# Fox layer of a two-layer trunk: the residual turned by VectorE's 32x32 blocks and transfers through DRAM, and added by VectorE, in place of transposes on TensorE

## The chip, the cores and the metric

The kernel runs on one core of one Trainium2 chip. The metric is the device time of one execution in microseconds (us), the median of several executions. The profile is of one further execution; its times count from the start of its span.

## What is computed

The reference is a decoder trunk of two pre-norm residual layers on a sequence of 1024 positions with 1024 features, all in float32: an RG-LRU layer, then an attention layer with a forget gate ("FoX"), then a final RMSNorm. What matters here is the end:

```python
def fox_mixer(h, w_in, b_f, w_out):
    ...                      # q, k, v, gate; softmax with a decay; o = p @ v per head
    y = o * jax.nn.silu(gate)
    return y @ w_out.astype(h.dtype)

x = x + fox_mixer(h, ...)    # second layer; x is the residual after the first
return rms_norm(x, final_g)  # over the features of each position
```

## The kernel before, in words

**Layout.** Through both layers the features lie on the 128 partitions and the positions run along a partition (`x` is held as 8 blocks `db` of 128 features, each for two halves `c` of 512 positions). The output is wanted the other way round, a position on a partition, so that the final norm sums along the partition. A product that must be exact to float32 is three matmuls of rounded parts (high times high, low times high, high times low): `hh`/`hl` and `wh`/`wl` are the high and low parts of an activation and of a weight.

**The attention layer.** The loop of lines 1127 to 1177 goes over 16 heads. For each half `c`, `maxima` (line 752) makes the scores `S` on TensorE, VectorE subtracts the mask and takes the row maximum, ScalarE takes the exponential; `weigh` (line 817) turns the weights (`pt`, on TensorE for the last heads), ScalarE and VectorE split them into `ph` and `pl`, and TensorE multiplies them with `v` into `O`. The sums of a head pass through DRAM: `rc` to `recd` (line 796), back broadcast to `recb` (line 805). GpSimd multiplies them into the gate (`scale`, line 810) and the gate into the head (`gated`, line 909), and `split_y` (line 986) splits the gated head.

**The output projection.** `y` has 8 blocks of 128 features, one for each pair of heads. The first 6 blocks are multiplied with `w_out` beside heads 14 and 15 by `partial` (line 1005): for each feature block `db` and half `c`, 16 in all, it loads the residual block `xp` from `x1d` in DRAM, makes a product of 18 matmuls in a PSUM bank (`ops` in the profile), has VectorE add the two (line 1016), and stores the sum over the residual in `x1d` (line 1017). The order is (db, c) = (0,0) (1,0) (0,1) (1,1) (2,0) ... (6,0) (7,0) (6,1) (7,1). The tag `R` has two buffers, so each `xp` is loaded when the store from the last but one is through.

The last two blocks wait for heads 12 to 15, and come out in the other layout: `turned` (line 1036) makes, for each of 8 blocks of 128 positions and 2 halves `h` of 512 features, a PSUM bank (`turn`) in which 4 transposes of the residual (`x`, loaded by `residual`, line 1023) and 6 matmuls with `y` as the stationary part are summed. These are 16 groups: 8 for c=0, of which three run among the last matmuls of head 15, and then 8 for c=1. For c=0 all groups use the two banks of tag `g`, which the `ops` use too; for c=1 the blocks alternate between the tags `g` and `O`, two banks each. Behind a group ScalarE squares and sums it (line 1066) and VectorE multiplies it with the gain `grow` (lines 1068, 1071). For c=1 each block's root mean (`root_mean`, line 1080) is taken at once and the block is scaled, half on ScalarE, half on VectorE (lines 1072, 1073); for c=0 `finish` (line 1192) takes one root for all four blocks and scales them beside the groups of c=1.

**What sets the order.** Each engine has one queue in order. The strings `ORDER` and `LAST` (lines 27, 28) and those in `run` say how the steps of a head (digits) and of the projection (dots, `fill`) are woven on TensorE; a scheduler then places every engine's instructions by its own estimate of times. All DMAs are issued by SyncE, in order: an issue that waits holds up those behind it.

## Time and profile before

| | |
|---|---|
| time, median of 3 runs | 1112.8 us (1111.73 to 1114.34) |
| profiled execution | 1113.33 us, its span 1111.6 us |
| TensorE matmul busy | 1088.2 us, 98% of the span |
| VectorE busy | 785.4 us, 71% |
| ScalarE busy | 581.3 us, 52% |
| GpSimd busy | 175.2 us, 16% |
| DMA | 145.8 MB, mean 131 GB/s |

The profiler's page names engines PE (TensorE), PEld (its weight loads, beside the matmuls), DVE (VectorE), ACT (ScalarE), POOL (GpSimd) and SP (SyncE). A row of the timeline is start, duration, engine, line, operation, output<-inputs, shape, and in brackets the idle time before it and what ended it. Matmuls follow one another before the row of the one ahead ends, so durations of matmuls overlap and what counts is the distance of their starts. A "line" can be that of a helper: all matmuls stand at line 57, all splits at lines 87 (high) and 98 (low). The granted clock is 1.00 from start to end but for the last 3 us.

### The profile page before, as it was taken

How to read it: one execution, taken by the hardware profiler on the slowest of the kernel's cores; microseconds unless marked ns; L12 is line 12 of the kernel's file. 1: busy time of each engine (PE TensorE's matmuls, PEld its weight loads, DVE VectorE, ACT ScalarE, POOL GpSimd, SP SyncE). 2: the span in 40 equal slices, each digit the busy share in tenths (PEclk: the TensorE clock that was granted, in tenths of full speed). 3: DMA queues.
4: the chain of work that ended last, by engine and by line, in shares of the span. 5: the costliest groups of instructions: out<-in, count | busy, mean ns of one | idle time of the engine just before them, and what ended most of it. 6: DMA issues, size and time to landing. Idle time of an engine off the chain costs nothing.

```text
span 1111.6 us, 15903 instructions
## 1 busy us (share of the span) xinstructions
PE 1088.2 (98%) x5645; PEld 921.9 (83%) x5645; DVE 785.4 (71%) x1280; ACT 581.3 (52%) x1037; POOL 175.2 (16%) x120
## 2 busy tenths in 40 slices
PE   9999999999999999999999999999999999999997
PEld 7787888888888888988888888888888889888876
DVE  7888755876568687757788477875678765666645
ACT  8487345355453665545555355553555544444435
POOL 2322212111212201420010200202002020110110
PEclk9999999999999999999999999999999999999999
DMA  6111111111112113446767347675376763885445
GB/s 220 62 52 43 51 54 48 43 54 45 49 45 75 48 55 127 130 113 165 199 204 195 116 139 195 198 198 146 107 204 195 202 170 100 251 294 182 138 148 189
DMA packets 100919, 145.81 MB, mean 131 GB/s; under 512 B 25348, under 2 KB 53636, under 8 KB 100840
## 3 DMA queue, kind: packets, MB, share of 16 engines
q1 hardware_dynamic: 100840, 144.80, 44.2%
q8 instruction: 44, 0.72, 0.3%
q14 instruction: 35, 0.29, 0.1%
HBM read 83.48 MB, written 36.11 MB: 108 GB/s over the span
## 4 chain that ended last, share of the span: by engine, by line
PE 75%; DMA 8%; DVE 7%; issue 5%; ACT 3%; SPq 1%; POOL 1%; ACTq 0%; DVEq 0%; POOLq 0%
PE gps L57 24%; PE ops L57 16%; PE ups L57 10%; PE vps L57 8%; PE O L57 5%; PE S L57 4%; PE gate L57 3%; PE turn L57 2%; DMA pp<-turnd 2%; PE pt L61 2%; DMA wf<-in_w 2%; DVE pl L98 2%; DMA turnd<-turn 1%; DVE turn L735 1%; DVE S L775 1%
## 5 line engine op out<-in xcount | busy, mean ns | idle before, releaser
L57 PE MATMUL gps<-hh,wh 128*128 128x512 f32 x576 | 229.8, 399 | 0.3 <-ACT wh L87 0.3
L57 PE MATMUL gps<-hh,wl 128*128 128x512 f32 x576 | 226.2, 393 | 0.0
L57 PE MATMUL gps<-hl,wh 128*128 128x512 f32 x576 | 225.3, 391 | 0.0
L87 ACT CAST wh<-wf 128x512 fp32r<-128x512 f32 (+2 forms) x156 | 94.5, 610 | 152.6 <-PE gps L57 47.8
L98 POOL TENSOR_TENSOR wl<-wf,wh 128x512 fp32r<-128x512 f32 (+1 forms) x60 | 101.9, 1705 | 376.0 <-ACT wh L87 261.4
L57 PEld LDWEIGHTS gps<-hl,wh 128*128 128x128 f32 x576 | 108.5, 188 | 23.5
L57 PEld LDWEIGHTS gps<-hh,wl 128*128 128x128 f32 x576 | 108.8, 189 | 19.6 <-POOL wl L98 0.2
L57 PEld LDWEIGHTS gps<-hh,wh 128*128 128x128 f32 x576 | 108.7, 189 | 19.4 <-ACT wh L87 0.6
L815 POOL TENSOR_TENSOR sg<-sg,recb 64x512 f32<-64x512 f32 x32 | 44.1, 1397 | 494.9 <-DMA recb<-recd 494.9
L775 DVE CUSTOM_DVE_ANT_0 S<-S,mask 128x512 f32<-128x512 f32 (+7 forms) x128 | 97.1, 758 | 25.4 <-PE S L57 24.9
L780 ACT ACTIVATE pp<-S,m 128x512 f32<-128x512 f32 (+1 forms) x64 | 54.4, 850 | 76.8 <-DVE m L775 76.3
L57 PE MATMUL S<-T,U 128*128 128x512 f32 (+7 forms) x384 | 91.4, 346 | 0.0
L57 PE MATMUL O<-pl,v 128*128 128x256 f32 (+3 forms) x302 | 80.3, 301 | 10.8 <-DVE pl L98 10.5
L98 DVE TENSOR_TENSOR wl<-wf,wh 128x512 fp32r<-128x512 f32 x96 | 64.9, 677 | 30.7 <-ACT wh L87 30.5
L375 DVE TENSOR_TENSOR x<-x,ops 128x512 f32<-128x512 f32 x80 | 54.1, 680 | 40.7 <-PE ops L57 40.7
L57 PE MATMUL O<-ph,v 128*128 128x256 f32 (+3 forms) x302 | 80.1, 289 | 1.3 <-ACT ph L87 1.3
L57 PEld LDWEIGHTS S<-T,U 128*128 128x128 f32 (+1 forms) x384 | 68.2, 189 | 12.6 <-ACT pp L780 0.6
L57 PE MATMUL ups<-hh,wl 128*128 128x512 f32 x192 | 75.3, 392 | 0.8 <-POOL wl L98 0.8
L57 PE MATMUL ups<-hh,wh 128*128 128x512 f32 x192 | 75.5, 394 | 0.4 <-ACT hh L89 0.4
L57 PE MATMUL ops<-yh,wh 128*128 128x512 f32 x192 | 75.2, 392 | 0.0
L57 PE MATMUL ups<-hl,wh 128*128 128x512 f32 x192 | 75.1, 391 | 0.1
L57 PE MATMUL ops<-yh,wl 128*128 128x512 f32 x192 | 74.7, 389 | 0.0
(170 smaller groups left out, 2361.8 us busy)
## 6 DMA issues: line engine op xcount, KB each, us to landing
wf<-in_w SPq DMA_DIRECT2D x100, 256.0 KB
turnd<-turn SPq DMA_DIRECT2D x26, 448.0 KB
pp<-turnd SPq DMA_DIRECT2D x52, 224.0 KB
wf<-in_wo SPq DMA_DIRECT2D x64, 128.0 KB
U<-qkh SPq DMA_DIRECT2D x64, 128.0 KB
T<-qkh SPq DMA_DIRECT2D x28, 256.0 KB
turnd<-turn SPq DMA_DIRECT2D x13, 384.0 KB
pp<-turnd SPq DMA_DIRECT2D x52, 96.0 KB
```

The source lines that it names most:

```text
L57: pe[0] = nc.tensor.matmul(*args, **kw)
L61: pe[0] = nc.tensor.transpose(*args)
L87: nc.scalar.copy(hi, src)
L98: return eng.tensor_tensor(lo, src, f32(hi), ALU.subtract)
L375: nc.vector.tensor_tensor(x, x, pt, ALU.add)
L735: nc.vector.transpose(t[:, 0 if c else r].rearrange("p (m k q) -> p k m q", m=4, q=32), p[:, :n].rearrange("p (k m q) -> p k m q", m=4, q=32),
L775: masked[0] = nc.vector.tensor_tensor_reduce(S[:, :n], S[:, :n], mask[:, SEQ - n :], -1.0, -NEG, ALU.add, ALU.min, accum_out=m)
L780: seen[0] = nc.scalar.activation(p, S[:, :n], AF.Exp, bias=m, scale=-1.0, accum_out=sums[:, i : i + 1])
L815: nc.gpsimd.tensor_tensor(sg, sg, recs[hd // 2][rows, part], ALU.mult)
```

## The change

`partial` no longer stores the sum in the old layout. VectorE adds the residual to the product in the PSUM bank itself, then turns it by its transpose of 32x32 blocks into the tile `x`, and four stores of 64 KB put the blocks into a new DRAM tensor `x2d` such that a position's row of features can be read back onto a partition. `fetch` loads them, 512 KB at a time, four for each half `c`; `fetch(0)` is placed ahead of the last product, `fetch(1)` behind head 15.

`turned` makes the bank of 6 matmuls alone; VectorE then adds the residual piece by piece (two additions of 256 columns for a group), from PSUM and SBUF into `res`. The square of ScalarE reads `res`. For c=0 the product with the gain goes to GpSimd, and `finish` scales one half on ScalarE, one on VectorE. For c=1 VectorE applies root and gain in one instruction for each half (line 1105 of the changed kernel). The last block of c=1 (`early`) is an exception: there TensorE adds the residual with an identity matrix in float32 (two matmuls of 256 columns for a group), and the rest is as before. The gain `grow` lies in two tiles of another pool, and its load stands earlier in SyncE's queue. The diff, cut to its core:

```diff
+    x2d = dram.tile([2, P, KT, 4, P], F32, name="x2d")
...
+                if (db, c) == todo[-1]:
+                    fetch(0)
...
-                nc.vector.tensor_tensor(x, x, pt, ALU.add)
-                nc.sync.dma_start(x1d[c, :, db], x)
+                nc.vector.tensor_tensor(pt, x, pt, ALU.add)
+                nc.vector.transpose(
+                    x.rearrange("p (b k d) -> p k b d", b=4, d=32), pt.rearrange("p (k b q) -> p k b q", b=4, q=32)
+                )
+                for m in range(4):
+                    nc.sync.dma_start(
+                        x2d[c, :, db, m].rearrange("(b q) f -> q b f", b=4),
+                        x[32 * m : 32 * m + 32].rearrange("q (b f) -> q b f", b=4),
+                    )
...
+        def fetch(c):
+            if c == 0:
+                x = [tu.tile([P, SEQ], F32, tag=t, name="x1") for t in ("U", "U0", "U1")]
+                x.append(at.tile([P, SEQ], F32, tag="sg", name="x1"))
+            else:
+                x = [tu.tile([P, 2, SEQ], F32, tag=f"T{h}", name="x1") for h in range(2)]
+                x = [z[:, i] for z in x for i in range(2)]
+            for d, z in enumerate(x):
+                nc.sync.dma_start(z, x2d[c, :, 2 * d : 2 * d + 2].rearrange("p e m f -> p (e m f)"))
+            rows_of[c] = x
...
-                    for i in range(4):
-                        x = xs[4 * h + i][:, b * P : (b + 1) * P]
-                        matmul(pt[:, i * P : (i + 1) * P], x, ident, start=i == 0, stop=False, is_transpose=True)
+                    pt = bank(b)
+                    if early:
+                        for i, (x, p) in enumerate(pieces(c, b, h, pt)):
+                            matmul(p, ident, x, start=i == 0, stop=False)
...
+                    src = pt
+                    if not early:
+                        src = res[h]
+                        for x, o, p in pieces(c, b, h, src, pt):
+                            nc.vector.tensor_tensor(o, x, p, ALU.add)
...
-                    nc.scalar.activation(sq, pt, AF.Square, accum_out=ss[:, h : h + 1])
+                    nc.scalar.activation(sq, src, AF.Square, accum_out=ss[:, h : h + 1])
+                    if c == 0:
+                        nc.gpsimd.tensor_tensor(src, src, grow[h], ALU.mult)
...
+                else:
+                    r = root_mean(ss)
+                    for z, g_ in zip(res, grow):
+                        nc.vector.scalar_tensor_tensor(z, z, r, g_, ALU.mult, ALU.mult)
...
-                nc.vector.tensor_scalar(o, o, r[:, i : i + 1], None, ALU.mult)
-                nc.sync.dma_start(out[i], o)
+                nc.scalar.activation(res[0], res[0], AF.Copy, scale=r_)
+                nc.vector.tensor_scalar(res[1], res[1], r_, None, ALU.mult)
+                for o, hs in zip(res, halves):
+                    nc.sync.dma_start(out[i, :, hs], o)
```

**VectorE around the last product.** `ops_10356` is the last product before, (7,1); the lines are: 906 a head's halves added, 98 a low part, 1016 the sum with the residual, 1068 the product with the gain.

```order
L906 TENSOR_TENSOR yo<-yo,O 64x256
L98 TENSOR_TENSOR yhl<-yo,yhh 128x256
L1016 TENSOR_TENSOR xp<-xp,ops_10356 128x512
L1068 TENSOR_TENSOR res<-turn,grow 128x512
L98 TENSOR_TENSOR pl<-pt,ph 128x512 x2
L1068 TENSOR_TENSOR res<-turn,grow 128x512
```

In the changed kernel the same product is `ops_10427`; the lines 907, 1019 stand for 906, 1016, line 1020 is the new transpose, line 1086 a new addition of 256 columns.

```order
L907 TENSOR_TENSOR yo<-yo,O 64x256
L98 TENSOR_TENSOR yhl<-yo,yhh 128x256
L1019 TENSOR_TENSOR ops_10427<-xp,ops_10427 128x512
L1020 STREAM_TRANSPOSE xp<-ops_10427 128x4x4x32
L1086 TENSOR_TENSOR res<-x_10417,turn 128x256
L1086 TENSOR_TENSOR res<-x_10418,turn 128x256
L1086 TENSOR_TENSOR res<-x_10419,turn 128x256
L1086 TENSOR_TENSOR res<-x_10420,turn 128x256
L98 TENSOR_TENSOR pl<-pt,ph 128x512 x3
```

The transpose, which reads the bank, stands behind the sum, and the additions of the first two groups stand ahead of the low parts `pl` where one product with the gain stood.

**VectorE at the end**, before, from the root of c=0 (`ssq_4013`) on; `ssq_4014` are the sums of c=1, line 1087 the reciprocal of a root, line 1073 a scaling by it.

```order
L1087 RECIPROCAL ssq_4013<-ssq_4013 128x4
L1197 TENSOR_SCALAR res<-res,ssq_4013 128x1024 x4
L1068 TENSOR_TENSOR res<-turn,grow 128x512
L1084 TENSOR_TENSOR ssq_4014<-ssq_4014 128x1
L1071 TENSOR_TENSOR res<-turn,grow 128x512
L1068 TENSOR_TENSOR res<-turn,grow 128x512
L1087 RECIPROCAL ssq_4014<-ssq_4014 128x1
```

The changed kernel's last rows; there `ssq_4015` are the sums of c=1, line 1105 is the scaling by root and gain, lines 1092, 1099 and 1101 belong to the last block.

```order
L1086 TENSOR_TENSOR res<-x_10624,turn 128x256 x2
L1114 TENSOR_TENSOR ssq_4015<-ssq_4015 128x1 x2
L1117 RECIPROCAL ssq_4015<-ssq_4015 128x1
L1105 SCALAR_TENSOR_TENSOR res<-res,ssq_4015,grow 128x512 x2
L1092 TENSOR_TENSOR res<-turn,grow 128x512
L1117 RECIPROCAL ssq_4015<-ssq_4015 128x1
L1114 TENSOR_TENSOR ssq_4015<-ssq_4015 128x1
L1099 TENSOR_TENSOR res<-turn,grow 128x512
L1105 SCALAR_TENSOR_TENSOR res<-res,ssq_4015,grow 128x512 x2
L1117 RECIPROCAL ssq_4015<-ssq_4015 128x1
L1101 TENSOR_SCALAR res<-res,ssq_4015 128x512
```

The scalings of the third block stand among the last block's instructions, ahead of its reciprocal.

**SyncE's queue around head 15's last sums**, before: line 1013 loads a residual block, line 1017 stores a sum, lines 1029 and 1033 load the residual for the groups.

```order
L1017 DMA x1d<-xp 128x512
L1013 DMA xp<-x1d 128x512
L1029 DMA x_10390<-x1d 128x256
L1033 DMA x_10582<-x1d 128x2x256
L796 DMA recd<-rc 4x128
L1033 DMA x_10514<-x1d 128x2x256
L805 DMA recb<-recd 64x512
```

And in the changed kernel, where line 1016 loads a residual block, line 1024 stores a turned sum, and line 1042 is `fetch`, with `x_10417` to `x_10420` for c=0 and `x_10623`, `x_10624` for c=1.

```order
L1024 DMA x2d<-xp 32x4x128 x4
L1042 DMA x_10419<-x2d 128x1024
L1042 DMA x_10624<-x2d 128x1024
L1016 DMA xp<-x1d 128x512
L1024 DMA x2d<-xp 32x4x128 x4
L797 DMA recd<-rc 4x128
L1042 DMA x_10420<-x2d 128x1024
L1016 DMA xp<-x1d 128x512
L806 DMA recb<-recd 64x512
L1024 DMA x2d<-xp 32x4x128 x8
L1042 DMA x_10624<-x2d 128x1024
```

Ahead of `recb` there now stand a fetch of 512 KB and a load, which wait for the four stores before them.

More of the change, by code (lines that the diff above doesn't have):

```diff
@@ new lines, in turned, with bank @@
+        def turned(c):
+            def bank(b):
+                return ps.tile([P, HALF], F32, tag="gO"[c * (b % 2)], name="turn")
+            homes = [(wpool, t) for t in ("wl", "wh") * 4]
+            if c:
+                homes = [(rpool, "R")] * 2 + [(at, t) for t in ("ph", "pl") * 3]
+            for b in range(4):
+                cs = slice(b * P, (b + 1) * P)
+                ss = ssq[c][:, 2 * b : 2 * b + 2]
+                early = c == 1 and b == 3
+                res = []
+                for h, hs in enumerate(halves):
+                    own, tag = homes.pop(0)
+                    kw = dict(bufs=3) if own is at else {}
+                    res.append(own.tile([P, HALF], F32, tag=tag, name="res", **kw))
+                    pt = bank(b)
+                    if early:
+                        for i, (x, p) in enumerate(pieces(c, b, h, pt)):
+                            matmul(p, ident, x, start=i == 0, stop=False)
@@ L1059, in turned @@
                         wh, wl = (z[:, k::2] for z in late_w[h])
-                        matmul(pt, yh, wh, start=False, stop=False)
+                        matmul(pt, yh, wh, start=k == 0 and not early, stop=False)
                         matmul(pt, yl, wh, start=False, stop=False)
@@ L1188, in trunk @@
         drain(fill)
-        for q in range(2):
-            left[1, q] = residual(1, q)
+        fetch(1)
         def finish():
```

64 lines of the change are left out of this document (25 added, 39 removed).

## The prediction

> **What bounds the kernel now.** I read the busy time by stage first, then TensorE's waits, then the chain that ended last, then the timeline of the last 50 us. Columns of the stages: length, and busy us (instructions) of PE, PEld, DVE, ACT and POOL, then granted clock, DMA share and GB/s.
>
> ```profile
> 480.00:960.00 480.00, 467.41 (x2685) 403.80 (x2684) 343.31 (x667) 243.30 (x530) 60.28 (x42) 1.00 0.63 171
> 960.00:1070.00 110.00, 110.00 (x571) 93.37 (x570) 65.37 (x132) 47.74 (x101) 10.24 (x8) 1.00 0.63 206
> ```
>
> From 960 to 1070 us, where the sixteen `ops1` products run beside heads 14 and 15, TensorE has no idle time at all and VectorE is busy 65.4 of 110 us. After 1070 the rest of the output projection runs in 16 groups (8 for c=0, 8 for c=1), each 4 transposes and 6 matmuls. There TensorE waits once, in the list of its waits from 960 us on:
>
> ```profile
> PE turn L57 <- DVE xp L1016: 1.7, 1, 1.7
> ```
>
> The chain of waits says what that wait hangs on (start, us, what), and how the end follows:
>
> ```profile
> 1064.31 3.51 DMA recd<-rc
> ...
> 1067.84 2.73 DMA recb<-recd
> ...
> 1073.72 0.70 DVE xp L1016
> ...
> 1074.46 1.35 PE turn L57 x7
> ...
> 1082.94 22.71 PE turn L57 x123
> ...
> 1107.32 0.72 ACT res L1072
> ```
>
> The softmax sums of head 15 travel through DRAM and land at 1070.57, GpSimd and ScalarE use them, VectorE splits the gated head, and only behind that in VectorE's order comes the addition that empties the PSUM bank of the last `ops1`. From 1074.46 on TensorE runs without a pause to 1105.64, and 6.0 us of tail (squares, root, scaling, transfer) follow to 1111.6. So 31 us are bound by TensorE, behind one fixed start.
>
> **What the change takes from TensorE.** The timeline of c=0's last groups, a row for each matmul:
>
> ```profile
> 1087.18 0.60 PE L57 MATMUL turn<-ident,x 128*128 128x128 f32 x4
> 1087.54 0.48 PE L57 MATMUL turn<-woh,yhh 128*128 128x512 f32 x1
> ...
> 1089.01 0.60 PE L57 MATMUL turn<-ident,x 128*128 128x128 f32 x4
> ...
> 1090.84 0.60 PE L57 MATMUL turn<-ident,x 128*128 128x128 f32 x4
> ```
>
> A group takes 1.83 us. Its 4 transposes take 0.36, and the first matmul behind them is some 0.08 late; six matmuls alone take 1.40. So 0.43 us go from each of 14 groups, 6.0 us. The last two groups keep the residual on TensorE, as two fp32 matmuls of 256 columns in place of four transposes. The nearest row is the fp32 matmul of 512 columns, two instructions, up to the start of what follows:
>
> ```profile
> 34.75 1.02 PE L57 MATMUL rsrow<-rs,onesf 128*128 128x512 f32 x2
> 35.61 0.95 PE L57 MATMUL sscol<-onesf,m 128*128 128x1 f32 x8
> ```
>
> That is 0.86 for 512 columns, so 0.86 for twice 256: 0.43 more than the transposes, 0.9 us for the two groups. TensorE's own saving is 5.1 us. What of it arrives at the end is the question.
>
> **What comes in ahead.** Sixteen VectorE transposes of 128x512 between 980 and 1075 us. The rows of the same operation at other lengths, and of the additions and scalings used below (busy, mean ns):
>
> ```profile
> L735 DVE STREAM_TRANSPOSE turn<-pp 128x896 f32<-128x896 f32 x26 | 28.8, 1110 | 8.3 <-ACT pp L780 8.1
> L735 DVE STREAM_TRANSPOSE turn<-pp 128x384 f32<-128x384 f32 x26 | 14.8, 568 | 2.1 <-ACT pp L780 2.1
> L98 DVE TENSOR_TENSOR wgl<-wgf,wgh 128x256 fp32r<-128x256 f32 x12 | 5.0, 414 | 0.0
> L1073 DVE TENSOR_SCALAR res<-res,ssq 128x512 f32<-128x512 f32 x4 | 1.9, 486 | 0.1
> ```
>
> A straight line through the first two gives 0.70 us at 512. That is 11.2 us more for VectorE, whose share in the stage goes from 0.59 to 0.70. TensorE waits on none of it directly; it would wait on what stands behind a transpose in VectorE's order, the low parts `pl`, the row maxima, the banks. The tightest place that I found is this: `pl` is done at 1000.82 and read at 1002.45.
>
> ```profile
> 1000.27 0.55 DVE L98 TENSOR_TENSOR pl<-pt,ph 128x384 fp32r<-128x384 f32 x1
> 1002.45 0.28 PE L57 MATMUL O<-ph,v 128*128 128x256 f32 x1
> ```
>
> Two transposes stand ahead of it in the new order, so some 1.1 to 1.4 us of the 1.6 are used up. The cost lies between 0 and 2.9 us: the stage 480 to 960, with VectorE at 0.72, lost 12.6 us of TensorE in 480, which over 110 us is 2.9. Below zero it can't go, since TensorE has no idle time there to win. I take 0.6, nearer to the margins I see than to that other stage, whose operations pass through DRAM as well.
>
> SyncE issues four stores in place of one for each product. Issues of the nearest shapes (ns, least/median/most):
>
> ```profile
> L747 SPq DMA_DIRECT2D pp<-turnd x104: 595/610/1459, 515.9 to 955.7; - x104
> L1017 SPq DMA_DIRECT2D x1d<-xp x16: 319/326/417, 987.9 to 1074.4; - x16
> ```
>
> Between 0.33 and 0.61 each; I take 0.5, so 2 us for a product where there were 0.33, every 5.9 us. SyncE has room for that. What matters is who stands ahead of `recb`, which starts the chain above: in the new order a 512 KB fetch, itself waiting for the stores of (7,0), and the last load of 256 KB. They go out at some 1065.5 and 1066, `recb` not before `recd` has landed at 1067.8. At the 414 GB/s that the last outputs reach (a row below) their 768 KB need 1.9 us, so `recb` is late by 0 to 1.9; having about 2 us of lead they are mostly through, and I take 0.3.
>
> **The bank and the first groups.** The bank that TensorE waits for is now free only after the addition and the transpose, one depending on the other: 1074.46 becomes 1075.2. The first group's 0.43 is swallowed by this wait, which grows from 1.7 to 3.0 us. Then, in the new VectorE order, the two additions of the second group stand ahead of the `pl` that the last quarter's `O` matmuls read. They wait for that group's last matmul (1077.5), end at 1078.45, and `pl` at 1079.1: TensorE, there at 1078.85, waits 0.25. So after the fourth group it stands at 1083.2 where it stood at 1083.53: nearly all that three groups save is gone. From there it gains 0.43 a group: end of c=0 at 1088.8 (1090.84 before), six groups of c=1 to 1097.2, two of 2.35 to 1101.9, 3.7 us earlier than 1105.64. A bank is free 0.9 us after a group's end (its last row ends 0.17 after the next could start, two additions of 256 columns at 0.33 and 0.41), in time for the group after next.
>
> **The tail.** Here I find a new bound. VectorE's rows in c=1 (start, us; neighbours that don't wait start 0.60 apart):
>
> ```profile
> 1094.28 0.18 DVE L1087 RECIPROCAL ssq<-ssq 128x4 f32<-128x4 f32 x1 [1.70 <-ACT ssq L1086]
> ...
> 1097.83 0.68 DVE L1071 TENSOR_TENSOR res<-turn,grow 128x512 f32<-128x512 f32 x1
> 1098.43 0.68 DVE L1068 TENSOR_TENSOR res<-turn,grow 128x512 f32<-128x512 f32 x1
> ...
> 1107.13 0.15 DVE L1087 RECIPROCAL ssq<-ssq 128x1 f32<-128x1 f32 x1
> ```
>
> Of ScalarE and of GpSimd:
>
> ```profile
> 1092.66 1.28 ACT L1086 ACT_TABLE_LOAD   x1 [0.87 <-DVE ssq L1084]
> ```
> ```profile
> 1061.37 1.29 POOL L915 TENSOR_TENSOR yo<-yo,sg 128x512 f32<-128x512 f32 x1 [12.22 <-DVE yo L906]
> ```
>
> The reciprocal for c=0 stood at 1094.28. It now needs the last square of c=0, and in ScalarE's order the first square of c=1 too (its additions end at 1091.15), then the table load of 1.28 and the root: 1093.6 (first square done at 1091.9, root 0.3). Behind it VectorE has, before the last reciprocal: 4 scalings of c=0 (1.7), 4 pairs of additions (3.0), 6 scalings by root and gain (3.7 at 0.61), 2 products with the gain (1.3), and 7 short ones (1.2), 10.9 us in all. Before it had 2.7 of scalings, 8 products at 0.6 (4.8) and 3 scalings of 512 (1.3), 8.8 in 12.7 us, with room between. So the queue is done at 1104.5 at the earliest; two waits for ScalarE's squares (of the sixth group of c=1, and of the last) add about 0.8: the last reciprocal at 1105.3 against 1107.13. ScalarE's own queue, with the 4 scalings of c=0's other halves between its squares, stays just ahead. GpSimd's eight products of c=0, at 1.29 us, end at 1091.8, before VectorE and ScalarE scale them; at twice that they would not.
>
> Behind the last reciprocal all is as before but for two more transfers of 256 KB close ahead of the last two, for which I add 0.1. The end is then 1.8 to 1.9 us earlier, not 3.7.
>
> **The sum.** -1.9 (tail), +0.6 (VectorE ahead of 1070), +0.3 (`recb`): -1.0 us. The profiled execution took 1113.33 us, 1.7 more than its span of 1111.6, and lies 0.5 above the median of 1112.8. I carry the difference to the median: 1111.8. Two runs of this kernel differ by up to 2.6 us, and I count a change under 0.2%, 2.2 us, as none.
>
> **The rivals.** *TensorE's end arrives in full.* If VectorE's queue in c=1 is shorter than my 10.9 us by 1.8 or more (additions that hide behind each other, squares that come sooner), the end follows TensorE: 3.7 less, with the 0.9 of losses 1109.9 to 1110.0, and 1109.1 without them. For it: in c=1 VectorE was busy only two thirds of the time before. Against it: the order leaves it no room after 1093.6.
>
> *The clock falls in the wait.* Granted clock after the last matmul (1105.64), in the column before the DMA share:
>
> ```profile
> 1108.50:1109.00 0.50, 0.00 (x0) 0.00 (x0) 0.00 (x0) 0.00 (x0) 0.00 (x0) 0.88 0.64 250
> 1109.00:1109.50 0.50, 0.00 (x0) 0.00 (x0) 0.00 (x0) 0.00 (x0) 0.00 (x0) 0.50 1.08 414
> ```
>
> The mean of 0.88 over the first half microsecond means that it fell to half at 1108.9, 3.2 us after the last matmul. The wait in front of the second group grows to 3.0, with `recb` late to 3.3: just there. If it falls, matmuls run at half speed for about as long again, 3.2 us, and 1.6 us are lost: 1113.4, no measurable change. For it: the two lengths are equal within my error. Against it: 1.7 us of idle did nothing.
> The Trainium skill has this as a rule against the change (TensorE: Matmul & The Clock Gate, section Part 1: The HAM clock gate): the clock is halved after an idle window of about 3.4 us, and a busy window of the same length gives it back. By that rule the loss would be 1.7 us, on a wait of 3.0 to 3.3 perhaps; the trace's 3.2 agrees with it, and no run here shows a wait of that length in the middle.
>
> *VectorE becomes the bound before 1070.* If the transposes fall in front of what TensorE is about to read, each can cost up to its 0.70, 11.2 us in all. Half of them on the path give 5.6: -1.9 + 0.3 + 5.6 = +4.0, 1116.8. It decides from 3.8 us of stalls on, seven transposes of sixteen. For it: TensorE has no idle time in that stage, so each stall counts, and a share of 0.72 cost 2.6% elsewhere. Against it: the margins of 1 us and more that I find. The transposes are gone from TensorE in any case; that the change doesn't do what it says is no case.
>
> **Chances.** Forecast 0.42 (range of its own 1109.5 to 1113.5, of which a quarter lies below 1110.6), TensorE's end in full 0.20, the clock 0.18 (a fifth of it beyond 2.2 us with other losses), VectorE before 1070 0.20. Faster by over 0.2%: 0.11 + 0.20 = 0.31. Slower: 0.04 + 0.20 = 0.24. Within: 0.45. The range takes the first three cases and the lower part of the fourth: 1109.0 to 1116.0.
>
> **What would show it.** Right: TensorE idle about 3 us before the second group, starting at 1075 to 1076; groups of 1.40; no new waits of TensorE in 960 to 1070; its last matmul near 1102 to 1103, with VectorE busy nearly without a gap from 1094 to the last reciprocal and a tail of 8 us or so instead of 6. Wrong: a tail of 6 us, waits `O <- pl` or `S` ahead of 1070, a granted clock under 1.00 about 1076 to 1080, or GpSimd's products ending after 1094.

## The result, and the profile after

The changed kernel takes 1119.87 us (median of 5, 1118.04 to 1122.14) against 1113.39 us for the kernel before (median of 5, 1111.73 to 1115.6): a ratio of 1.006, 95% interval 1.0042 to 1.0077. It is slower by 6.5 us by the medians, where the prediction had -1.0. The profiled execution took 1120.34 us, its span 1118.6 us, 7.0 more than the span before.

The two stages of before, in the changed kernel (columns as there: length, busy us of PE, PEld, DVE, ACT and POOL, granted clock, DMA share, GB/s):

```profile
480.00:960.00 480.00, 468.50 (x2702) 405.22 (x2701) 342.66 (x673) 245.12 (x535) 60.85 (x43) 1.00 0.63 173
960.00:1070.00 110.00, 105.12 (x530) 87.41 (x529) 69.74 (x138) 45.00 (x96) 10.17 (x8) 0.98 0.67 209
```

Up to 960 TensorE's busy time differs by 1.1 us in 480. From 960 to 1070 TensorE, which had no idle time, now has 4.9 us of it, and the granted clock is no longer 1.00. TensorE's waits from 960 us on, where there was one of 1.7 us:

```profile
PE turn L57 <- DVE xp L1020: 3.6, 1, 3.6
PE pt L61 <- DVE pl L98: 2.7, 2, 2.3
PE S L57 <- ACT pp L781: 2.2, 2, 2.0
PE turn L57 <- DVE res L1086: 0.2, 1, 0.2
```

Four marks show where the 7 us lie: on TensorE the scores `S` near 997, the last `S` and the start of the second group, and on VectorE the last reciprocal. Timeline of before (its second group and its last reciprocal stand in the prediction):

```profile
996.90 0.40 PE L57 MATMUL S<-T,U 128*128 128x256 f32 x2
...
1055.96 0.76 PE L57 MATMUL S<-T,U 128*128 128x320 f32 x4
```

After, on TensorE:

```profile
994.75 0.40 PE L57 MATMUL S<-T,U 128*128 128x256 f32 x2
...
1061.52 0.76 PE L57 MATMUL S<-T,U 128*128 128x320 f32 x4
...
1081.48 0.79 PE L57 MATMUL turn<-woh,yhh 128*128 128x512 f32 x1 [3.64 <-DVE xp L1020]
```

and on VectorE:

```profile
1114.14 0.15 DVE L1117 RECIPROCAL ssq<-ssq 128x1 f32<-128x1 f32 x1
```

From `S` to the last `S` it took 59.06 us and takes 66.77 (+7.7); from there to the second group 18.50 and 19.96 (+1.5); from there to the last reciprocal 32.67 and 32.66 (0.0). These are +9.2; the span is only 7.0 longer, because this execution stood 2.15 us ahead at the first mark. Of these 1.7 are a stretch at half clock in the profile of before, which neither the tenths on its page nor the table of before show. So the clock of before was not at 1.00 up to the last 3 us, as was said ahead of the prediction:

```profile
620.00:625.00 5.00, 4.27 (x19) 3.54 (x19) 4.95 (x6) 2.09 (x7) 3.97 (x3) 0.66 0.56 142
```

**Where the 7.7 us went.** The chain of waits of the changed kernel ahead of the wait for `S` (start, us, what):

```profile
1036.77 0.24 SPq L1024
...
1037.05 0.43 SPq L1024
...
1037.53 0.45 SPq L1024
...
1038.02 5.07 DMA x2d<-xp
...
1043.11 3.52 DMA xp<-x1d
...
1046.72 0.10 DVE ops L1019
...
1047.93 0.63 DVE xp L1020
1048.55 0.57 DVE yo L907
1049.13 1.15 DVE S L776
...
1051.38 0.20 ACT pp L781
```

It does not run through TensorE at all. Four stores of a turned tile are issued one by one; the last lands 5.07 us after its issue; only then may the next `xp` be loaded into that tile, 3.52 us; the addition waits for it at the head of VectorE's queue, and behind it stand the transpose, a sum of `O` and the row maximum for which ScalarE and then TensorE wait. SyncE's own queue shows the other half of the circle:

```profile
1036.58 1.96 SPq L1024 DMA_DIRECT2D x2d<-xp  x4
1043.11 0.34 SPq L1016 DMA_DIRECT2D xp<-x1d  x1
1043.55 0.38 SPq L1042 DMA_DIRECT2D x<-x2d  x1
1044.02 1.84 SPq L1024 DMA_DIRECT2D x2d<-xp  x4
1048.75 0.34 SPq L1016 DMA_DIRECT2D xp<-x1d  x1
```

The load at 1043.11 waits for the four stores of 1036.58, and the next four stores, whose transpose was done at 1039.2, stand behind it until 1044.02. So the next load comes late as well.

The wait of 2.3 us near 997 comes from the same circle, earlier on. Eight stores were issued one by one from 987.78 on, the load that the addition needs went out behind them and behind `recb` at 992.59, and VectorE stood waiting for it, 4.93 us, ahead of the low parts `pl` that TensorE reads:

```profile
987.78 3.72 SPq L1024 DMA_DIRECT2D x2d<-xp  x8
...
996.32 0.70 DVE L1019 TENSOR_TENSOR ops<-xp,ops 128x512 f32<-128x512 f32 x1 [4.93 <-DMA xp<-x1d]
```

**What the wait costs on top.** The granted clock (the column before the DMA share) around the waits of 2.0 and 3.6 us:

```profile
1052.50:1053.00 0.50, 0.50 (x4) 0.40 (x3) 0.50 (x2) 0.50 (x3) 0.00 (x0) 0.70 0.00 0
1053.00:1056.00 3.00, 3.00 (x9) 2.33 (x8) 3.00 (x7) 0.35 (x2) 1.18 (x1) 0.50 0.39 112
1056.00:1056.50 0.50, 0.50 (x4) 0.42 (x3) 0.43 (x1) 0.50 (x1) 0.09 (x1) 0.89 0.00 0
...
1080.00:1080.50 0.50, 0.00 (x0) 0.00 (x0) 0.50 (x1) 0.00 (x0) 0.00 (x0) 0.51 0.00 0
1080.50:1086.50 6.00, 5.02 (x16) 4.24 (x17) 1.88 (x6) 1.80 (x4) 1.27 (x1) 0.50 0.30 85
1086.50:1087.00 0.50, 0.50 (x3) 0.35 (x2) 0.50 (x3) 0.07 (x1) 0.00 (x0) 0.67 0.79 287
```

From the means of the edge slots it was at half from 1052.70 to 1056.11 (3.4 us, 1.7 lost) and from 1080.01 to 1086.83 (6.8 us, of which 5.35 lie behind the start of the second group: up to 2.7 lost). The 7.7 us are then waits of 2.3 and 0.4 (`pt`), 2.0 and 0.2 (`S`), 1.7 of clock, and 1.1 that these rows leave open.

**The second group** hangs on the same chain as before, and `recb` is its slow part:

```profile
1071.01 0.34 SPq L1042
...
1071.40 0.42 SPq L1016
...
1071.92 4.91 DMA recb<-recd
```

4.91 us instead of 2.73, right behind a fetch of 512 KB and a load of 256 KB.

### The profile page after: what moved, and what is told of

It reads as the page before. It is cut to its first block, busy times and chain, and to the rows that moved or that the text cites. A ratio compares the mean times of both kernels' runs of the same rounds, so it can differ in the third digit from the quotient of the medians.

```text
span 1118.6 us, 15910 instructions
## 1 busy us (share of the span) xinstructions
PE 1086.7 (97%) x5589; PEld 918.2 (82%) x5589; DVE 797.3 (71%) x1313; ACT 581.1 (52%) x1038; POOL 183.0 (16%) x128
## 4 chain that ended last, share of the span: by engine, by line
PE 68%; DMA 11%; DVE 9%; issue 5%; ACT 3%; SPq 2%; POOL 1%; DVEq 0%; ACTq 0%; POOLq 0%
PE gps L57 24%; PE ops L57 13%; PE ups L57 10%; PE vps L57 8%; PE O L57 4%; PE S L57 3%; PE gate L57 2%; DMA pp<-turnd 2%; DMA wf<-in_w 2%; DVE pl L98 2%; PE pt L61 2%; DMA x2d<-xp 1%; DMA turnd<-turn 1%; DVE S L776 1%; DVE turn L736 1%
## 5 line engine op out<-in xcount | busy, mean ns | idle before, releaser
L98 POOL TENSOR_TENSOR wl<-wf,wh 128x512 fp32r<-128x512 f32 (+1 forms) x60 | 99.5, 1663 | 379.0 <-ACT wh L87 262.4
```

Source lines behind the costliest of these rows:

```text
L98: return eng.tensor_tensor(lo, src, f32(hi), ALU.subtract)
```

## The experiments

The theory with which I went into them: the stage ahead of 1070 is held up by the circle of stores and loads (theory A below); the first rival is that the transposes themselves take VectorE away (theory B). All ratios are against the kernel before, on the same chip in the same session; a difference in us in the text is the ratio's. The last three columns are the distances between the marks in the profile of one execution: `S` to last `S`, last `S` to the second group, second group to last reciprocal.

| kernel | median us | before | ratio (95%) | S to S | to 2nd group | to reciprocal |
|---|---|---|---|---|---|---|
| before | | | | 59.06 | 18.50 | 32.67 |
| changed | 1119.87 | 1113.39 | 1.006 (1.0042 to 1.0077) | 66.77 | 19.96 | 32.66 |
| plain_store | 1115.10 | 1112.64 | 1.0022 (1.0006 to 1.0038) | 60.99 | 19.29 | 31.73 |
| no_turn_four | 1117.28 | 1112.64 | 1.0045 (1.0028 to 1.0062) | 61.14 | 19.13 | 31.73 |
| no_turn_plain | 1114.97 | 1112.64 | 1.0022 (1.0003 to 1.0041) | 60.49 | 18.90 | 30.15 |
| own_tile | 1119.08 | 1112.64 | 1.005 (1.0031 to 1.0069) | 63.69 | 19.68 | 31.72 |
| load_shuffle | 1117.11 | 1113.20 | 1.0031 (1.0019 to 1.0043) | 61.77 | 19.65 | 31.74 |
| pool_stores | 1119.71 | 1113.20 | 1.0047 (1.0032 to 1.0061) | 64.54 | 19.91 | 30.14 |
| warm | 1118.91 | 1113.20 | 1.005 (1.0033 to 1.0066) | 64.57 | 20.89 | 31.78 |
| no_turn_plain_warm | 1112.49 | 1113.20 | 0.9987 (0.9974 to 1.0000) | 61.04 | 19.30 | 30.18 |
| own_pool | 1110.44 | 1113.53 | 0.9974 (0.9961 to 0.9987) | 59.39 | 16.50 | 30.12 |
| load_shuffle_own | 1119.21 | 1113.53 | 1.0046 (1.0029 to 1.0063) | 62.84 | 20.06 | 31.74 |
| fetch_behind | 1119.42 | 1113.53 | 1.0049 (1.0030 to 1.0068) | 67.20 | 18.03 | 30.11 |
| best | 1113.10 | 1113.53 | 0.9998 (0.9982 to 1.0014) | 63.24 | 17.53 | 30.06 |
| order_only | 1117.74 | 1113.03 | 1.003 (1.0013 to 1.0047) | 65.38 | 16.68 | 30.18 |
| own_tile_order | 1110.93 | 1113.03 | 0.996 (0.9944 to 0.9976) | 59.40 | 16.50 | 30.13 |
| load_shuffle_own_order | 1111.44 | 1113.03 | 0.9975 (0.9962 to 0.9989) | 60.28 | 16.50 | 30.21 |
| before_order | 1113.71 | 1113.03 | 0.9998 (0.9983 to 1.0012) | 59.17 | 16.64 | 32.59 |

Two executions of one kernel differ by up to 8 us (order_only: 1113.95 to 1122.17), so a profile's distances say where time goes, and the ratio of the medians whether it does so as a rule.

### Stores, transposes, tail and tile, one by one

**plain_store.** One plain store in place of the four:

```diff
-                for m in range(4):
-                    nc.sync.dma_start(x2d[c, :, db, m]..., x[32 * m : 32 * m + 32]...)
+                nc.sync.dma_start(x2d[c, :, db].rearrange("p m f -> p (m f)"), x)
```

> The four stores of a turned tile become one store of 256 KB whose rows land in another layout, so the residual of the result is wrong; the sixteen VectorE transposes, all additions and the tail stay. Theory A (the loop: a load of `xp` stands in SyncE's queue behind four stores of the tile before, and waits until the four stores of its own tile have landed, so additions in VectorE's order come late and hold `pl` and the row maxima): TensorE's waits of 2.3 and 2.0 us near 997 and 1050 and the clock window behind the second are gone, 5 to 6 us earlier than with four stores, 1113 to 1115 or +0 to +1.5 against before. Theory B (the transposes themselves, 11.4 us of VectorE in front of what TensorE reads): no change from 1119.9, the waits stay.

Measured: +2.4 us, 0.9 above theory A's range, and 4.2 below the changed kernel. The waits near 997 and 1050 are gone, `S` to `S` is 60.99. What is left of waits in the stage, with all sixteen transposes, is 0.8 us.

**no_turn_four.** No transposes, the four stores left:

```diff
-                nc.vector.tensor_tensor(pt, x, pt, ALU.add)
-                nc.vector.transpose(x.rearrange(...), pt.rearrange(...))
+                nc.vector.tensor_tensor(x, x, pt, ALU.add)
```

> The sixteen VectorE transposes are left out (the sum is added in place in the loaded tile and stored unturned, so the residual is wrong); the four stores of 64 KB each stay. Theory A (the loop of stores and loads): the waits near 997 and 1050 stay, 1117 to 1120. Theory B (the transposes): back to 1112 to 1114.

Measured: +5.0 us (median 1117.28), in theory A's range. The profiled execution (1115.91) is one of the fastest of ten; its waits ahead of 1065 are 1.0 and 0.4 us where they were 2.3 and 2.0. So the four stores carry most of the loss without the transposes. In the profiles the two together cost more than both alone: 7.7 us in the stage, against 1.9 and 2.1 with either left out and 1.4 without both.

**no_turn_plain.** Both edits: only the tail is the changed one.

> Neither transposes nor four stores: the sum is added in place and stored by one transfer, as in the kernel before, and only the tail is the changed one (the residual is wrong, being unturned). Stage ahead of 1070 as before. By the prediction's terms the tail alone is worth -1.9 and a late `recb` +0.3: -1.6, about 1111.5 to 1112. If the tail's gain is only enough to pay what the clock loses in the wait before the second group, as the second start to the last reciprocal took 32.7 us in both profiles, -0.5 to +0.5 against before. If `recb` is late by 2 us here too, +1 to +2.

Measured: +2.4 us, just above the last of the three, but from ten executions between 1111.4 and 1119.27, and not for the reason given there (`recb` took 2.81 us). The profiled one is the fastest, and in it the clock stays at 1.00 to the last matmul:

```profile
1075.05 0.50 PE L57 MATMUL turn<-woh,yhh 128*128 128x512 f32 x1 [2.57 <-DVE xp L1019]
...
1105.20 0.16 DVE L1110 RECIPROCAL ssq<-ssq 128x1 f32<-128x1 f32 x1
```

That is 30.15 us, 2.5 less than before. Over the ten, the mean granted clock is 0.998 in the two fastest and 0.993 to 0.997 in the others. That would fit a tail that is worth its gain, and a clock that takes it back in most executions; no_turn_plain_warm, below, tests it.

**own_tile.** The transposes write to a tile of their own, in two buffers idle at that time, so that a load of `xp` waits only for the addition:

```diff
+                t = at.tile([P, HALF], F32, tag="xp", name="xt", bufs=2)
                 nc.vector.transpose(
-                    x.rearrange(...), pt.rearrange(...)
+                    t.rearrange(...), pt.rearrange(...)
```

> The transposes write to a tile of their own (two buffers that lie idle in this stage), so that the load of `xp` waits only for the addition that read the tile, not for four stores to land; four stores and all transposes stay. Theory A (the loop): loads of `xp` are issued 2 to 5 us earlier, the waits near 997 and 1050 shrink to under 1 us in all, 1114 to 1116. Theory B (the transposes): 1118 to 1121. If SyncE's issues alone (four for one, in order ahead of the loads of weights and sums) are the cost, whatever the tiles: 1117 or more too, with the loads still late by the issues.

Measured: +5.6 us, against theory A and in the range of theory B, which plain_store had already spoken against. Yet the circle is broken: no addition waits for a load any more. What TensorE waits for now, ahead of 1070:

```profile
PE O L57 <- DVE pl L98: 1.1, 1, 1.1
PE O L57 <- ACT ph L87: 1.1, 1, 1.1
```

SyncE issues `recd` at 989.57, and then two loads and eight stores ahead of `recb`, at 995.74: 6.17 us between them where before had 2.98 (987.15 and 990.13). And VectorE's order makes TensorE pay for it:

```profile
1004.53 0.69 DVE L98 TENSOR_TENSOR yhl<-yo,yhh 128x512 fp32r<-128x512 f32 x1 [3.54 <-ACT yhh L87]
1005.15 0.42 DVE L98 TENSOR_TENSOR wl<-wf,wh 128x256 fp32r<-128x256 f32 x1
1005.48 0.71 DVE L1021 STREAM_TRANSPOSE xt<-ops 128x512 f32<-128x512 f32 x1
1006.11 0.52 DVE L98 TENSOR_TENSOR pl<-pt,ph 128x384 fp32r<-128x384 f32 x1
```

`yhl`, the split of a gated head that hangs on `recb`, stands ahead of the `pl` that TensorE reads next, and VectorE sits idle for 3.54 us in front of it. Behind the two waits of 1.1 us the clock is at half for 3.4 us; with the 1.7 us that this takes they make 3.9 of the 4.6 us that `S` to `S` is longer. So there was a second way to the same stall, hidden behind the first.

### Fetches, queues and the clock

**load_shuffle.** A turned tile is stored by one transfer of 2 KB rows; each fetch becomes four:

```diff
-                for m in range(4):
-                    nc.sync.dma_start(x2d[c, :, db, m]..., x[32 * m : 32 * m + 32]...)
+                nc.sync.dma_start(x2d[c, db].rearrange("m q b f -> (m q) (b f)"), x)
...
-                nc.sync.dma_start(z, x2d[c, :, 2 * d : 2 * d + 2]...)
+                src = x2d[c, 2 * d : 2 * d + 2].rearrange("e m q b f -> b q (e m) f")
+                for b in range(4):
+                    nc.sync.dma_start(z[32 * b : 32 * b + 32]..., src[b])
```

> The whole change, but the regrouping of partitions moves from the stores to the fetches: each turned tile is stored by one transfer of 2 KB rows, and each fetch of 512 KB becomes four of 128 KB with 512-byte rows; the result is the full one. In the place of 64 stores and 8 fetches stand 16 and 32. Theory A2 (what costs is SyncE's queue: four issues of 0.45 us for a product, in order ahead of the loads of `xp` and of `recb`): most of what four stores cost comes back, +2 to +4 against before, near the 1115.1 of the single plain store. Theory B2 (what costs is moving the residual in 512-byte rows, wherever it is done): +5 to +7, as the whole change.

Measured: ratio 1.0031, +3.5 us, in A2's range and not in B2's.

**pool_stores.** `nc.gpsimd.dma_start` for the four stores.

> The four stores of each turned tile are issued from GpSimd's queue, all else is the whole change; the result is the full one. Theory A2 (SyncE's queue): TensorE's waits near 997 and 1050 are gone and `recb` of head 15 is issued as early after `recd` as before; +2 to +4 against before. Theory B2 (the transfers themselves): the waits stay, +5 to +7. A third way: GpSimd is slow at issuing or is held by a store that waits for its transpose, and its own products of the gate come late: over +7.

Measured: ratio 1.0047, +5.2 us: B2's number, but not its cause. With SyncE free the shared tile still makes the circle: a store landing after 4.88 us and the load behind it 2.83 us in the middle of the stage, and at the end the last load:

```profile
1077.54 4.22 DMA xp<-x1d
...
1081.86 0.16 DVE ops L1019
```

GpSimd needs 0.55 us for each of these issues.

**warm.** The first group's six matmuls are done three times, in the wait ahead of the second:

```diff
+                    for k in (0, 1) * 2 * (c == b == h == 0):
+                        ...   # the same 3 matmuls as below, start at k == 0, stop at k == 1
                     for k in range(2):
```

> The whole change, and the first group's six matmuls are done three times over (each time from a fresh start, so the result is the full one): 12 more matmuls, 2.8 us of TensorE in the wait of 3.6 us before the second group. Theory C (the clock falls in that wait, and half speed costs 2.6 us of the tail): the granted clock stays at 1.00 from 1076 to 1100, and 2 to 3 us come back, +3.5 to +5 against before. If the clock costs nothing because VectorE bounds the tail anyway: no change, +6 to +7.

Measured: ratio 1.005, +5.6 us, not theory C's +3.5 to +5, if only just. The wait shrank to 1.8 us, and the clock fell all the same, for 3.4 us from 1082 on: 31.78 to the last reciprocal. One stretch at half instead of two.

**no_turn_plain_warm.** The same 12 matmuls in no_turn_plain.

> The new tail alone (sum in place, one plain store, no transposes, so the residual is wrong), with the same 12 matmuls more in the wait before the second group, which was 2.6 us. Theory C (without the clock's fall the tail is worth the -1.9 of the prediction; its executions from 1111.4 to 1119.3 differ by falls of the clock): -1 to -2.5 against before and a narrow spread. If something else in the tail costs 2 us: +1.5 to +2.5 as without the matmuls.

Measured: ratio 0.9987, -1.4 us, twelve executions within 1110.82 to 1114.16, mean granted clocks of 0.995 to 0.999. Here the wait is only 0.3 us. As theory C has it: with useless matmuls in the wait the kernel is 3.5 per thousand faster than without (0.9987, 1.0022, each against the kernel before on its own chip).

### Both ways shut, and the order

**own_pool.** own_tile and pool_stores together.

> The whole change, with both earlier edits at once: the transposes write to a tile of their own and the four stores are issued from GpSimd's queue; the result is the full one. Theory D (two ways lead to the same stalls: a load of `xp` waits until the stores of its tile have landed, and `recb` and the loads stand behind the stores' issues on SyncE; each edit alone shut one of them and gained 1 us or less, +5.0 per mille and +4.7 per mille against before): with both shut +1 to +3 us, TensorE's waits ahead of 1065 under 1.5 us in all. Rival E (the 512-byte rows, or the amount that is moved, hold up whatever else is in transit): +5 to +6, as each alone. GpSimd's own queue (2.2 us of issues for a product, at times in front of the gate's products) may cost up to 2 of it; then the waits are for `O` and `turn`.

Measured: ratio 0.9974, -2.9 us: faster than before, and 4 us better than the nearer end of theory D. `S` to `S` is 59.39, and TensorE's only wait up to the second group is 0.2 us. One thing that I hadn't counted on may explain the surplus, and the last four runs test it: the scheduler had placed three rows differently. VectorE's order in own_tile and own_pool, at the three places where `yhl` stands otherwise (on ScalarE `yhh` and `ph` change places with it):

```
own_tile                         own_pool
yhl<-yo,yhh 128x512              (wl, transpose)
(wl, transpose)                  pl<-pt,ph 128x384
pl<-pt,ph 128x384                yhl<-yo,yhh 128x512
...
yhl<-yo,yhh 128x512              pl<-pt,ph 128x384
pl<-pt,ph 128x384                addition, transpose of (6,1)
addition, transpose of (6,1)     yhl<-yo,yhh 128x512
...
yhl<-yo,yhh 128x256              addition, transpose of (7,1)
addition, transpose of (7,1)     additions of the first group
additions of the first group     yhl<-yo,yhh 128x256
```

**load_shuffle_own.** own_tile in load_shuffle.

> One plain store for a product, four fetches in place of one, and a tile of its own for the transposes; SyncE issues everything; the result is the full one. Theory D: both ways are shut, TensorE's waits ahead of 1065 under 1.5 us, +1 to +2.5 us against before, of which 1 to 1.5 are halves of the clock in the wait before the second group. Rival E: as the fetches with 512-byte rows alone, +3.5.

Measured: ratio 1.0046, +5.1 us: against theory D. Only one issue for a product stands on SyncE, yet `yhl` still holds up `pl`, for 1.1 us: `recb` goes out 4.32 us after `recd` (986.34, 990.66) where before had 2.98, and GpSimd's two products with it take 2.99 us where they took 2.54. In the order of own_tile a little lateness is enough.

**fetch_behind.** One row of SyncE's queue moved: the last fetch for c=0 behind `recb` of head 15 (`tc.issue_after` on the instruction that loads `recb`).

> The whole change with one row of SyncE's order moved: the last fetch of 512 KB for c=0 is issued right behind `recb` of head 15 instead of ahead of it. Theory F (`recb` took 4.9 us instead of 2.7 because that fetch and the load of 256 KB were in transit): `recb` takes 3 to 3.5 us, the second group starts 1.4 to 2 us sooner after the last `S`, the time is 1 to 2 us less than the whole change, +4.5 to +5.5 against before. Rival (the fetch isn't what delays it, the 256 KB and the stores are): `recb` still 4.5 us or more, +6.5.

Measured: last `S` to second group 18.03 instead of 19.96, so theory F's 1.9 us are there in the profile, and the wait is 1.7 us as before the change; that fetch is the only row moved. `recb`, issued at 1075.09, is used by GpSimd from 1078.58 on, 3.5 us later, where it was 5.0 (1071.92, 1076.96). The ratio, 1.0049, is 1.2 us better than the changed kernel's, less than the two intervals could tell apart.

**best.** load_shuffle_own, fetch_behind, and the six matmuls twice.

> What the experiments point to, together: one plain store for a product and four fetches in place of one, transposes into a tile of their own, the last fetch behind `recb`, and the first group's six matmuls done twice (a fresh start each time), 1.4 us of TensorE in the wait before the second group; the result is the full one. By theories C, D and F: stage ahead of 1065 +0.5 to +1.5, wait before the second group as long as before the change, clock 1.00, the tail 2.5 us shorter: -0.5 to -2 us against before. If the clock falls in other places or the stage loses as before: +1 to +3.

Measured: ratio 0.9998, no change, worse than expected: the stage is 4.2 us longer than before, with the waits of load_shuffle_own (`S` 1.5, `O` 1.1).

So what told own_pool from the rest was open: SyncE's issues, or the order. Four more runs:

**order_only, own_tile_order, load_shuffle_own_order, before_order.** The three `yhl` are put behind those rows with `tc.issue_after`, and the first `yhh` on ScalarE behind the next `ph`; nothing else moves on TensorE, VectorE and ScalarE, and on SyncE only one load of weights, behind the next stores.

```diff
-                with tc.issue_after(seen[0].ins):
+                with tc.issue_after(seen[0].ins), tc.issue_after(pls[0].ins), tc.issue_after(phs[0].ins):
                     split_y(0, 6, yos[6, 0])
...
+                turned_ = nc.vector.transpose(...)
+                if (db, c) == todo[-2]:
+                    with tc.issue_after(turned_.ins):
+                        to_lo(yl, y, yh, nc.vector)
```

> The whole change with only the order moved on VectorE (three rows: `yhl` of head 13's pair behind the next `pl`, `yhl` of head 15's first half behind the addition and transpose of (6,1), `yhl` of its first quarter behind those of (7,1) and the first group's additions) and on ScalarE (`yhh` behind the next `ph`); four stores on SyncE and the shared tile stay; the result is the full one. Theory D (loop and SyncE's issues): the loop is left, so its waits near 1030 to 1050 stay: +3.5 to +6 against before. Theory G (the order is what lets a late `recb` hold TensorE): no wait near 997, none before the second group but for the last load of `xp`: +1 to +3.

Measured: ratio 1.003, +3.3 us: half of the loss is gone, and the half that the shared tile makes stays: waits of 2.0 (`pt`) and 1.2 us (`S`) ahead of 1065. The wait before the second group is 0.4 us.

> The transposes have a tile of their own, the four stores stay on SyncE, and the order is moved as in the run before this; the result is the full one. Theory G: -1 to -3 us against before, as with the stores on GpSimd. Theory D (SyncE's issues cost by themselves, through late loads): +2 to +5, with waits of TensorE ahead of 1065 as without the moved order.

Measured: ratio 0.996, -4.5 us (2.1 by the medians of 8 and 31 executions), at or beyond the good end of theory G; its interval overlaps own_pool's. Its four stores are issued by SyncE like those of own_tile, with which it shares everything but the order (and that one load of weights). TensorE's waits from 960 us to the end:

```profile
PE turn L57 <- DVE xt L1037: 0.2, 1, 0.2
PE turn L57 <- DVE res L1106: 0.2, 1, 0.2
```

And the row that held up `pl`, now behind it. It still waits, 2.13 us, but nothing that TensorE needs stands behind it:

```profile
999.78 0.52 DVE L98 TENSOR_TENSOR pl<-pt,ph 128x384 fp32r<-128x384 f32 x1
1002.43 0.69 DVE L98 TENSOR_TENSOR yhl<-yo,yhh 128x512 fp32r<-128x512 f32 x1 [2.13 <-ACT yhh L87]
```

> One plain store for a product, four fetches in place of one, a tile of its own, and the moved order; the result is the full one. Theory G: -1 to -3 us against before (+5.2 without the moved order). Theory D without G: unchanged, +3 to +5.

Measured: ratio 0.9975, -2.8 us, from +5.1 by the order alone: theory G.

> The kernel before, with the same moves of order (`yhl` behind the next `pl` and behind the last additions, `yhh` behind the next `ph`) and nothing else; the result is the full one. The only wait of TensorE after 960, 1.7 us in front of the second group, hangs on this order: it goes, -1 to -2 us against before. Then of the 3.1 us that the best kernel so far gained, only 1 to 2 are the change's own. If the wait is put elsewhere (the last quarter's `O` or the last groups wait for the later `yhl`): -0.5 to +0.5.

Measured: ratio 0.9998. In the profile TensorE has no wait at all after 960, and the second group starts 16.64 us after the last `S` instead of 18.50, the 1.9 us expected. The twelve times don't show it (1111.09, the profiled one, to 1115.5); an interval of 0.9983 to 1.0012 leaves room for 1.9 us and no more. This is not settled. What is settled is that the order gives the kernel before at most 2 per thousand, and the changed one 3 (shared tile), 7 (one plain store, own tile) and 9 (own tile). Most of own_tile_order's 4 would then be the change's own.

**What follows.** The change costs 6.5 us as it was made, and wins 2 to 4.5 with a tile of its own for the transposes and three rows of VectorE moved. Of the four combinations of tile and order only one is fast: shared and old 1.006, shared and moved 1.003, own and old 1.005, own and moved 0.996. The part of the order is the cleaner one of the two: with the tile of its own the scheduler also moved an addition and a row maximum on VectorE by a few rows, which no run separates from the tile.

## Why the prediction was wrong, point by point

**What bounds the kernel**: right, TensorE with one fixed start; and each stall of TensorE ahead of 1070 did count in full.

**TensorE's saving**: right. A group of six matmuls takes 1.36 us (1.40 predicted), the last two groups with their fp32 additions 2.25 (2.35).

**VectorE's durations**: right or close. Transposes of 0.71 (predicted 0.70), additions of 256 columns 0.41, scalings by root and gain 0.70 apart (predicted 0.61):

```profile
L1020 DVE STREAM_TRANSPOSE xp<-ops 128x512 f32<-128x512 f32 x16 | 11.4, 712 | 0.3
L1019 DVE TENSOR_TENSOR ops<-xp,ops 128x512 f32<-128x512 f32 x16 | 11.1, 692 | 11.6 <-DMA xp<-x1d 8.4 <-PE ops L57 3.0
...
L1105 DVE SCALAR_TENSOR_TENSOR res<-res,ssq,grow 128x512 f32<-128x512 f32 x6 | 4.2, 746 | 0.1
```

**What comes in ahead: this step failed.** "SyncE has room for that": I compared 2 us of issues with the 5.9 us of a product, and that sum is right (0.44 an issue by the median). What I left out is the way round: four issues, the landing (1.75 to 5.07 us), a load that may be issued only then because it reuses the tile, its landing (2.25 to 3.96 us), the addition; and that the stores of the next product stand behind that load in the same queue. In the second row above the end of the way is to be read: the additions waited 8.4 us for loads of `xp`, where before it was 1.8. The same step looked at what a transpose holds up by its own length ("two transposes stand ahead of it"), and not at what an addition holds up that waits. I put 0.6 on this stage, with 2.9 as its upper bound; it cost 7.7 in the profile, 1.7 of them clock. My bound came from a stage with the same VectorE share; the share says nothing on a wait at the head of a queue. Two of the signs that I had named for being wrong came true here: waits for `S` ahead of 1070, and a granted clock under 1.00.

**`recb` late by 0.3**: the mechanism was named (a fetch of 512 KB and a load of 256 KB ahead of it), its size was not: 2.2 us, beyond my bound of 1.9. I let both be through after 2 us of lead; they were issued 0.9 and 0.5 us ahead of it. With the fetch behind `recb` 1.9 us came back.

**The bank and the first groups**: 0.7 us for the transpose in front of the second group, as measured. The wait became 3.6 instead of 3.0, by `recb`.

**The tail**: right. I had the second group at 1075.2 and the last reciprocal at 1105.3, 30.1 us; it is 30.06 to 30.21 wherever the clock holds. With a stretch at half it is 31.7, with two 32.66: the whole gain of 2.5 us was spent. The mechanism is there too, and not only the number: in own_tile_order the last matmul starts at 1097.88 and the last reciprocal only at 1101.59, and from 1090.23 on VectorE is never idle for more than 0.8 us. One slip of mine is in the sum: from 1107.13 to 1105.3, less 0.1 for the transfers, is 1.7, and I carried 1.9.

**The clock falls in the wait**: I gave it 0.18, and it happened, twice. I had taken 3.2 us of idle for the point from which it falls; but it fell behind waits of 2.0 and 1.8 us as well. As a rival it had one place and a price of 1.6; it cost 1.7 near 1054 and 2.5 behind 1081.

**VectorE becomes the bound before 1070**: its number, 1116.8, was nearest, its mechanism was not what happened. own_tile_order has all sixteen transposes and no wait of TensorE over 0.2 us. Its threshold was miscounted as well: 3.8 us of stalls at 0.70 are between five and six transposes, not seven.

## What to carry to other kernels

When a step that reuses a buffer gets slower stores, add up the whole way round (issues, landing, reload, use) and compare it with the period at which the buffer comes back, not the issue time with the queue's free share; then ask what stands behind the waiting instruction in its engine's queue. When a stall has two causes, taking away one can show little: the tile and the order each had to be tried with the other already mended. Two kernels that differ in one line can differ in the rows that a scheduler places, so compare the orders before giving the line the credit.

## What the runs showed of the hardware that was not expected

- The granted clock fell without a wait of 3 us. Here it fell 1.1 us after a wait of 2.0 us was over (1051.62, 1052.70), and 0.8 us after one of 1.8 us (1081.22, 1082.05 in warm); in own_tile after two waits of 1.1 us shortly behind one another. It did not fall after waits of 2.3 us (996.5, changed kernel) and 2.57 us (no_turn_plain, this execution). The lengths at half were 3.41 and 6.82 us, one to two. The Trainium skill (TensorE: Matmul & The Clock Gate, Part 1: The HAM clock gate) has a free-running window of about 3.4 us; the lengths agree. That a whole window must be idle does not agree with 1.8 and 2.0 us.
- Why equal waits differ can be read from the same profiles. Within each of the 18, all changes of the clock lie whole multiples of 3.41 us apart: in the changed kernel it falls at 1052.70, 1080.01 and 1114.14, the last two 8 and 10 times 3.41 us behind the one before. So the span can be cut into stretches of 3.41 us with known borders, and what counts is TensorE's idle time within one stretch. The wait of 2.0 us lay whole between 1049.29 and 1052.70; the longer one of 2.3 us was cut by the border at 998.09 into 1.55 and 0.77. From 10 us on, over the 18 profiles, no stretch with under 1.26 us of idle ended in a fall, and each at full clock with 1.97 us or more did (27 of them); between 1.26 and 1.92 us, 8 did and 16 did not.
- In the chain of the changed kernel the same transfer of 64 KB lands after 1.75 to 5.07 us; the longest had a fetch of 512 KB and a load of weights issued 2.4 and 1.9 us ahead of it. In pool_stores, all 64 of them took 1.9 to 7.1 us, with a median of 2.8. That what else is in transit makes the difference is not shown by a run of its own.
- An issue of such a store takes 0.44 us on SyncE by the median and 0.55 us on GpSimd; once tile and order were mended, the times don't tell the two apart (own_pool 0.9974, own_tile_order 0.996).
